# Every second chunk of a stationary-weight block runs its low-half matmuls first

## The chip, the cores and the metric

One NeuronCore of a Trainium2 chip runs the kernel. The metric is the device time of one execution in microseconds. Three runs of the kernel before gave 1018.92, 1020.08 and 1020.14 us; the median is 1020.08 us.

## The reference

The kernel computes one layer of a bidirectional encoder for a sequence of 256 positions and 2048 channels, in float32. The parts that matter here:

```python
h = _rms_norm(x, norm_g)
proj = jnp.einsum('bsd,dn->bsn', h, w_in)          # 2048 -> 16400 columns
q_p, k_p, v_p, o_p, za_p, gif_p, xb_p, zb_p, ga_p, gb_p = jnp.split(proj, cuts, axis=-1)
ya = _mlstm_branch(q_p, k_p, v_p, o_p, za_p, gif_p, b_if, head_g)     # 4 heads
yb = _rglru_branch(xb_p, zb_p, conv_w, conv_b, w_rg, b_rg, lam)       # recurrence over time
ya = jnp.einsum('bsw,wd->bsd', ya, w_branch_a)
yb = jnp.einsum('bsw,wd->bsd', yb, w_branch_b)
merged = sigmoid(ga_p) * ya + sigmoid(gb_p) * yb
return _rms_norm(x + jnp.einsum('bsd,de->bse', merged, w_out), final_g)
```

Nearly all of the work is in the large products. All weights are read once from HBM.

## The kernel before

**Precision by halves.** A float32 product is made of products in a shorter format (fp32r). Each operand is split into a high half (a cast on ScalarE) and a low half (what is left, a subtraction on VectorE). high x high, high x low and low x high are added up in PSUM.

**Chunks.** Weights come in chunks of 128 x 1024 values (512 KB). `load_chunk` issues the DMA on SyncE into a `raw` tile, casts it into a `whi` tile on ScalarE (line 135) and subtracts into a `wlo` tile on VectorE (line 136). There are six `raw` buffers and four each of `whi` and `wlo`. A cast waits until TensorE has done with the `whi` tile of four chunks before.

**The helper that the change touches** is `half_tr` (lines 295 to 309). It makes half a block, 256 transposed output columns, in four chunks (`kq` 0 to 3), with the weights as the stationary operand and the normalised input as the moving one. The input lies in the tile `sHL` with high and low half side by side, 2 x 256 columns for each of 16 slices of the contraction. A chunk has 8 weight tiles of 128 x 128 (4 slices, 2 halves of the output `m`). Before, each chunk runs 8 matmuls with the high halves of the weights (line 302; 512 columns, as they meet both halves of the input) and then 8 with the low halves (line 305; 256 columns, only the input's high half). Here the former are called wide, the latter narrow. Both add into the same PSUM pair `acc`. At the end `fold` (line 311) empties it: a copy on ScalarE (line 315) and an add on VectorE (line 317).

`half_tr` is called 22 times, 88 chunks: for the second to fourth of the query and key blocks (six calls, `qk_block`), for the x-branch of the recurrence in `rg_block(j)` (two calls for each head j, line 667), and for its gate blocks (eight calls, line 881).

**What stands around it.** Heads 0 to 3 come one after the other: `rg_block(j)`, then `head(j)`, which makes the head's v block (`block_nat`, lines 150 to 152) and its o and z blocks (`pair`, lines 166 to 169). Side work is hung between chunks by `tick()`, by lists named in `PLAN`: the convolution, gates and scans of the recurrence (line 736: multiply, 737: multiply, 741 and 743: scans over time), and of the head the product with the scores (line 819), its square and scale (ScalarE line 823, POOL lines 824 and 825, the result `sq`), the multiply with it (VectorE line 826) and the transposes of the result (line 834). Line 799 is a multiply of two gates that this product needs.

**What sets the order.** The Tile framework writes the order of each engine's instructions when the kernel is built: it plays the program through with its own estimate of times and takes, on each engine, what is ready, by priority. Code inside `urgent()` (the loads, casts and subtractions of chunks, and `fold`) has a high priority. On the chip each engine runs its list in that order and waits at semaphores. A change of two loops can therefore move side work on every engine.

Of the kernel before, what the change touches and what calls it, by code (L numbers as in the profile page):

```python
# [15 lines left out]
P = 128  # L16
S = 256
D = 2048
KT = D // P
# [14 lines left out]
            P=('g2 g3',),  # L34
# [12 lines left out]
def hybrid_encoder(ctx: ExitStack, tc: tile.TileContext, x, xt, pk, bif, fg, wg, wi, wr, wa, wb, wo, out):  # L47
    nc = tc.nc
    pe, act, dve, pool, sp = nc.tensor, nc.scalar, nc.vector, nc.gpsimd, nc.sync
# [17 lines left out]
    def sl(tag, dt=F32, cols=4096):  # L67
        return slot.tile([P, cols], dt, tag=tag, name=name("s" + tag))
# [3 lines left out]
    def aux(i=None):  # L72
        if i is None:
            i = auxn[0] % 4
            auxn[0] += 1
        return paux.tile([P, NB], F32, tag=f"aux{i}", name=name("aux"))

    def acc_pair():
        t = pacc.tile([P, 2 * NB], F32, tag="acc", name=name("acc"))
        return [t[:, :NB], t[:, NB:]], t  # L80
# [16 lines left out]
    def tick():  # L97
        if queue:
            c = queue.pop(0)
            if c is not None:  # L100
                c()
        for lane in lanes:
            for c in lane.pop(0) if lane else ():
                c()
# [12 lines left out]
    def load_chunk(src, dst=None, tag="w", bufs=4, parts=1, between=()):  # L117
        with urgent():
            raw = wp.tile([P, KC * NB], F32, tag="raw", name=name("raw"), bufs=6)
            if dst is None:  # L120
                hi = wp.tile([P, KC * NB], F32R, tag=tag + "hi", name=name(tag + "hi"), bufs=bufs)
                lo = wp.tile([P, KC * NB], F32R, tag=tag + "lo", name=name(tag + "lo"), bufs=bufs)
            else:
                hi, lo = dst
            w = KC * NB // parts
            for i in range(parts):
                r = slice(i * w, (i + 1) * w)
                last_dma[0] = (act if between and i == 0 else sp).dma_start(raw[:, r], src[:, r]).ins
                if i == 0:
                    first_dma[0] = last_dma[0]  # L130
            for i in range(parts):
                r = slice(i * w, (i + 1) * w)
                if i < len(between):
                    between[i]()
                last_copy[0] = act.copy(hi[:, r], raw[:, r]).ins  # L135
                last_sub[0] = dve.tensor_sub(lo[:, r], raw[:, r], f(hi[:, r])).ins  # L136
        return hi, lo

    def block_nat(src, xhi, xlo):
        ps, _ = acc_pair()  # L140
        for kq in range(KT // KC):
            tick()
            hi, lo = load_chunk(src[kq])
            for kk in range(KC):
                k = kq * KC + kk
                wh, wl = hi[:, kk * NB:(kk + 1) * NB], lo[:, kk * NB:(kk + 1) * NB]
                for tb in range(2):
                    o = k * S + tb * P
                    a, b = xhi(o, o + P), xlo(o, o + P)
                    pe.matmul(ps[tb], a, wh, start=(k == 0), stop=False)  # L150
                    pe.matmul(ps[tb], a, wl, start=False, stop=False)  # L151
                    pe.matmul(ps[tb], b, wh, start=False, stop=(k == KT - 1))  # L152
        return ps
# [141 lines left out]
    def half_tr(src, half, after=None):  # L295
        ps, both = acc_pair()
        for kq in range(4):
            tick()
            hi, lo = load_chunk(src[half * 4 + kq])
            tiles = [(kq * 4 + kk, m, kk * S + m * P) for kk in range(4) for m in range(2)]  # L300
            for k, m, o in tiles:
                pe.matmul(ps[m], hi[:, o:o + P], hl_t[:, 2 * k * S:2 * (k + 1) * S],  # L302
                          start=(k == 0), stop=False, skip_group_check=True)
            for k, m, o in tiles:
                pe.matmul(ps[m][:, :S], lo[:, o:o + P], hhi(k * S, (k + 1) * S),  # L305
                          start=False, stop=(k == KT - 1), skip_group_check=True)
            if after:
                after(kq)
        return both.rearrange("p (m q s) -> p m q s", m=2, q=2)
# [24 lines left out]
    hl_t = sl("HL", F32R, 8192)  # L334

    def hhi(a, b):
        return hl_t[:, a + a // S * S:a + a // S * S + b - a]
# [251 lines left out]
    def qk_block(blk, key, i, pre=()):  # L589
        ps = block_first(wi[blk], hhi, hlo, pre) if pre else None  # L590
        for m in range(2):
            r = slice(m * NB, (m + 1) * NB)
            if ps:
                v = ps[m]
            else:
                v = hp.tile([P, 2 * NB], F32, tag="to" if m == 0 else "zz", name=name("kt"))[:, :NB]
                fold(v, half_tr(wi[blk], m))
            if m == 0:
                qkh[key] = sl(f"C{i}", F32R, 1024)
                qkl[key] = sl(f"D{i}", F32R, 1024)  # L600
            if key[0] == "k":
                if i == 1:
                    drain_to(r_row)
                with urgent():
                    v3 = v.rearrange("p (m s) -> p m s", m=2)
                    dve.tensor_mul(v3, v3, rbc2)
            evac_split(qkh[key][:, r], qkl[key][:, r], v)
# [57 lines left out]
    def rg_block(j):  # L665
        for i in range(2):
            both = half_tr(wi[BLK_XB + j], i, h_renew if j == 0 and i == 1 else None)
            if j == 0 and i == 1:
                drain()
                rg["hs"] = sl("E")  # L670
            v = xp[:, 2 * i:2 * i + 2, 2:S + 2]
            fold(v, both)
            if j == 0:
                with urgent():
                    dve.tensor_mul(v, v, rbc2)
# [203 lines left out]
    for j in range(4):  # L879
        for i in range(2):  # L880
            both = half_tr(wi[BLK_ZB + j], i)
            if i == 0:
                zt = hp.tile([P, 2 * NB], F32, tag="zz" if j else "vhi", name=name("zt"))
                sg = hp.tile([P, 2 * NB], F32, tag="to" if j else "vlo", name=name("sg"))
            fold(zt[:, i * NB:(i + 1) * NB], both)
        act.activation(sg, zt, AF.Sigmoid)
        dve.tensor_mul(zt, zt, hs[:, j * 1024:(j + 1) * 1024])
        dve.tensor_mul(sg, sg, zt)
        ybh.append(sl(f"C{j}", F32R, 1024))
        ybl.append(sl(f"D{j}", F32R, 1024))  # L890
        act.copy(ybh[j], sg)
        dve.tensor_sub(ybl[j], sg, f(ybh[j]))
        if j == 0:
            fm_t.append(sl("PT", F32R))
        if j == 0:
            drain()
        for kq in (2 * j, 2 * j + 1):
            if kq in k_yb:
                form("b", kq, k_yb.index(kq), full=sg[:, (kq % 2) * NB:(kq % 2 + 1) * NB])
        if j == 1:  # L900
            early[0]()
# [83 lines left out]
    ps = block_nat(wo[2], mh, ml)  # L985
# [21 lines left out]
    for tb, a, b, col in ((0, 0, NB, 3), (1, 0, S, 3), (1, S, NB, 4)):  # L1007
        ps = aux()[:, :b - a]
        for k in range(KT):
            hi, lo = ch[k // KC]  # L1010
            c = (k % KC) * NB
            wh, wl = hi[:, c + a:c + b], lo[:, c + a:c + b]
            o = k * S + tb * P
# [79 lines left out]
```

## Time and profile before

| | |
|---|---|
| median of three runs | 1020.08 us (1018.92 to 1020.14) |
| the profiled execution | 1019.4 us |
| its span, first to last instruction | 1017.7 us |
| TensorE busy | 1009.0 us, 99%, 5076 matmuls |
| VectorE busy | 861.5 us, 85% |
| ScalarE busy | 620.4 us, 61% |
| DMA | 199.34 MB, mean 196 GB/s |

The busy time of a matmul in the trace is its whole way through the array, and matmuls overlap. What one costs in a dense stream is the distance from its start to the start of the next one. In the chain of waits the pieces are set end to end, so there the rows give these distances summed over a run.

### The profile page before, as it was taken

What the parts mean: (1) busy time and instruction counts of PE and PEld (TensorE: products, weight loads), DVE (VectorE), ACT (ScalarE), POOL (GpSimd) and SP (SyncE); (2) the same over time, 40 slices, a digit from 0 to 9 for tenths busy, and PEclk for the clock granted to TensorE, in tenths of its full rate; (3) what the DMA queues carried; (4) which work ended last, traced back from release to release, by engine and by line L of the source; (5) the groups of instructions that cost most, each with busy time, mean ns of one, the idle gap of its engine ahead of it and who ended that gap; (6) DMA issues with size and microseconds to landing.
All of it is one profiled execution on the core that took longest, in us unless ns stands there. A gap on an engine that the chain in (4) does not pass through costs nothing.

```text
span 1017.7 us, 13732 instructions
## 1 busy us (share of the span) xinstructions
PE 1009.0 (99%) x5076; PEld 858.1 (84%) x5076; DVE 861.5 (85%) x1139; ACT 620.4 (61%) x817; POOL 15.9 (2%) x35
## 2 busy tenths in 40 slices
PE   9999999999999999999999999999999999999997
PEld 9988888888888888888888888888888888888886
DVE  6777798689769976997798899997998988999993
ACT  7545476776586759576955565655655656455662
POOL 1000000010001000100000000000000000000000
PEclk9999999999999999999999999999999999999999
DMA  9764545646654566566556556566565656567452
GB/s 355 276 189 142 166 144 190 199 150 191 202 186 165 189 207 184 169 193 214 170 181 211 167 185 228 188 207 205 186 222 195 210 186 206 200 243 290 167 191 83
DMA packets 56100, 199.34 MB, mean 196 GB/s; under 512 B 6368, under 2 KB 6880, under 8 KB 55648
## 3 DMA queue, kind: packets, MB, share of 16 engines
q1 hardware_dynamic: 55168, 197.13, 58.1%
q10 hardware_dynamic: 864, 1.32, 0.4%
q8 instruction: 40, 0.66, 0.3%
q14 instruction: 28, 0.23, 0.1%
HBM read 196.33 MB, written 2.10 MB: 195 GB/s over the span
## 4 chain that ended last, share of the span: by engine, by line
PE 97%; DVE 2%; DMA 1%; issue 0%; ACT 0%; DVEq 0%
PE acc L302 16%; PE acc L166 14%; PE acc L168 14%; PE acc L169 14%; PE acc L305 8%; PE acc L150 4%; PE acc L151 4%; PE acc L152 4%; PE aux L166 3%; PE aux L168 3%; PE aux L169 3%; PE aux L819 1%; PE acc L292 1%; PE acc L290 1%; PE acc L291 1%; PE aux L704 1%
## 5 line engine op out<-in xcount | busy, mean ns | idle before, releaser
L136 DVE TENSOR_TENSOR wlo<-raw,whi 128x1024 fp32r<-128x1024 f32 (+1 forms) x290 | 348.3, 1211 | 82.3 <-ACT whi L135 81.1
L135 ACT CAST whi<-raw 128x1024 fp32r<-128x1024 f32 (+1 forms) x290 | 299.4, 1044 | 191.0 <-PE acc L169 69.4
L302 PE MATMUL acc<-sHL,whi 128*128 128x512 f32 x704 | 178.1, 393 | 0.0
L168 PE MATMUL acc<-wlo,sHL 128*128 128x512 f32 x444 | 173.0, 390 | 0.0
L169 PE MATMUL acc<-whi,sHL 128*128 128x512 f32 x444 | 172.8, 389 | 0.0
L166 PE MATMUL acc<-whi,sHL 128*128 128x512 f32 x444 | 170.6, 389 | 0.0
L302 PEld LDWEIGHTS acc<-sHL,whi 128*128 128x128 f32 x704 | 126.9, 189 | 23.2
L305 PEld LDWEIGHTS acc<-sHL,wlo 128*128 128x128 f32 x704 | 96.0, 190 | 7.2
L305 PE MATMUL acc<-sHL,wlo 128*128 128x256 f32 x704 | 99.2, 283 | 0.0
L166 PEld LDWEIGHTS acc<-whi,sHL 128*128 128x128 f32 x444 | 83.4, 188 | 17.2
L169 PEld LDWEIGHTS acc<-whi,sHL 128*128 128x128 f32 x444 | 83.4, 188 | 17.1
L168 PEld LDWEIGHTS acc<-wlo,sHL 128*128 128x128 f32 x444 | 83.4, 188 | 17.0
L172 ACT CAST whi<-t 128x1024 fp32r<-128x1024 f32 x61 | 64.1, 1052 | 50.7 <-PE acc L169 23.6
L173 DVE TENSOR_TENSOR wlo<-t,whi 128x1024 fp32r<-128x1024 f32 x61 | 74.3, 1219 | 14.0 <-ACT whi L172 13.5
L151 PE MATMUL acc<-wlo,sHL 128*128 128x512 f32 x160 | 62.6, 391 | 0.0
L150 PE MATMUL acc<-whi,sHL 128*128 128x512 f32 x160 | 62.5, 390 | 0.0
L152 PE MATMUL acc<-whi,sHL 128*128 128x512 f32 x160 | 62.4, 390 | 0.0
L173 DVE TENSOR_TENSOR wlo<-raw,whi 128x1024 fp32r<-128x1024 f32 x34 | 41.5, 1221 | 14.7 <-ACT whi L172 14.5
L172 ACT CAST whi<-raw 128x1024 fp32r<-128x1024 f32 x34 | 35.8, 1052 | 27.2 <-PE acc L169 15.7
L172 ACT CAST b<-raw 128x512 fp32r<-128x512 f32 x27 | 16.8, 621 | 34.5 <-DMA raw<-wi 18.9
L168 PE MATMUL acc<-wlo,sA 128*128 128x512 f32 x92 | 36.0, 392 | 0.0
L169 PE MATMUL acc<-whi,sB 128*128 128x512 f32 x92 | 35.9, 390 | 0.0
(363 smaller groups left out, 1694.8 us busy)
## 6 DMA issues: line engine op xcount, KB each, us to landing
raw<-wi SPq DMA_DIRECT2D x254, 512.0 KB, 4.1
raw<-wb SPq DMA_DIRECT2D x32, 512.0 KB, 4.1
raw<-wa SPq DMA_DIRECT2D x32, 512.0 KB, 4.2
raw<-wo SPq DMA_DIRECT2D x32, 512.0 KB, 4.7
raw<-wr SPq DMA_DIRECT2D x8, 512.0 KB, 4.2
sB<-x SPq DMA_DIRECT2D x4, 512.0 KB, 7.8
sA<-x SPq DMA_DIRECT2D x1, 2048.0 KB, 7.7
sA<-xt SPq DMA_DIRECT2D x7, 256.0 KB, 5.5
```

The costliest lines, as they stand in the source:

```text
L135: last_copy[0] = act.copy(hi[:, r], raw[:, r]).ins
L136: last_sub[0] = dve.tensor_sub(lo[:, r], raw[:, r], f(hi[:, r])).ins
L150: pe.matmul(ps[tb], a, wh, start=(k == 0), stop=False)
L151: pe.matmul(ps[tb], a, wl, start=False, stop=False)
L152: pe.matmul(ps[tb], b, wh, start=False, stop=(k == KT - 1))
L166: pe.matmul(ps, a, wh, start=id(ps) not in began, stop=False)
L168: pe.matmul(ps, a, wl, start=False, stop=False)
L169: pe.matmul(ps, b, wh, start=False, stop=stop)
L172: act.copy(hi, v)
L173: dve.tensor_sub(lo, v, f(hi))
L302: pe.matmul(ps[m], hi[:, o:o + P], hl_t[:, 2 * k * S:2 * (k + 1) * S], start=(k == 0), stop=False, skip_group_check=True)
L305: pe.matmul(ps[m][:, :S], lo[:, o:o + P], hhi(k * S, (k + 1) * S), start=False, stop=(k == KT - 1), skip_group_check=True)
```

## The change

The two loops over a chunk's tiles become one, which runs once for the high halves and once for the low halves. For `kq` 0 and 2 the high halves come first, as before; for `kq` 1 and 3 the low halves do. The last matmul into the PSUM pair is now a high one, so `stop` moves there. Nothing else is edited; the code below the place stands two lines further down (line 302 becomes 304, 305 becomes 307, later lines L become L + 2).

```diff
-            for k, m, o in tiles:
-                pe.matmul(ps[m], hi[:, o:o + P], hl_t[:, 2 * k * S:2 * (k + 1) * S],
-                          start=(k == 0), stop=False, skip_group_check=True)
-            for k, m, o in tiles:
-                pe.matmul(ps[m][:, :S], lo[:, o:o + P], hhi(k * S, (k + 1) * S),
-                          start=False, stop=(k == KT - 1), skip_group_check=True)
+            for high in (True, False) if kq % 2 == 0 else (False, True):
+                for k, m, o in tiles:
+                    if high:
+                        pe.matmul(ps[m], hi[:, o:o + P], hl_t[:, 2 * k * S:2 * (k + 1) * S],
+                                  start=(k == 0), stop=(k == KT - 1), skip_group_check=True)
+                    else:
+                        pe.matmul(ps[m][:, :S], lo[:, o:o + P], hhi(k * S, (k + 1) * S),
+                                  start=False, stop=False, skip_group_check=True)
```

In the order that the framework writes, the engines' lists change as follows. The numbers in the names are those of the buffers; `wlo_N+1` is the low half of the chunk whose high half is `whi_N`.

First, TensorE in the gate blocks, two chunks and a half of one half block. Before:

```order
L302 MATMUL acc_5041<-sHL_90,whi_5043 128x512 x8
L305 MATMUL acc_5041<-sHL_90,wlo_5044 128x256 x8
L302 MATMUL acc_5041<-sHL_90,whi_5065 128x512 x8
L305 MATMUL acc_5041<-sHL_90,wlo_5066 128x256 x8
L302 MATMUL acc_5041<-sHL_90,whi_5087 128x512 x8
```

and now:

```order
L304 MATMUL acc_5041<-sHL_90,whi_5043 128x512 x8
L307 MATMUL acc_5041<-sHL_90,wlo_5044 128x256 x8
L307 MATMUL acc_5041<-sHL_90,wlo_5066 128x256 x8
L304 MATMUL acc_5041<-sHL_90,whi_5065 128x512 x8
L304 MATMUL acc_5041<-sHL_90,whi_5087 128x512 x8
```

Narrow runs of two chunks stand side by side, and so do wide ones.

Second, TensorE at the end of the x-branch of head 0, where `acc_2246` is its second half block and `acc_2373` the v block of the head; `to_1961` is the tile whose transposes go to `aux_2471` and `aux_2480`. Before:

```order
L302 MATMUL acc_2246<-sHL_90,whi_2322 128x512 x8
L305 MATMUL acc_2246<-sHL_90,wlo_2323 128x256 x8
L302 MATMUL acc_2246<-sHL_90,whi_2344 128x512 x8
L305 MATMUL acc_2246<-sHL_90,wlo_2345 128x256 x8
L150 MATMUL acc_2373<-whi_2376,sHL_90 128x512
L151 MATMUL acc_2373<-wlo_2377,sHL_90 128x512
```

and now:

```order
L304 MATMUL acc_2246<-sHL_90,whi_2322 128x512 x8
L307 MATMUL acc_2246<-sHL_90,wlo_2323 128x256 x8
L150 MATMUL acc_2373<-whi_2376,sHL_90 128x512
L836 MATMUL aux_2471<-ident,to_1961 128x128
L836 MATMUL aux_2480<-ident,to_1961 128x128
L307 MATMUL acc_2246<-sHL_90,wlo_2345 128x256 x8
L304 MATMUL acc_2246<-sHL_90,whi_2344 128x512 x8
L151 MATMUL acc_2373<-wlo_2377,sHL_90 128x512
```

One matmul of the v block and two transposes now stand ahead of the last chunk, and its low half comes first.

Third, VectorE at the same place. Before:

```order
L743 SCALAR_TENSOR_TENSOR sC_399_1975<-sC_398_1974,sD_400_1976 128x256 x4
L826 SCALAR_TENSOR_TENSOR to_1961<-aux_2138,sq_2132,zz_1962 128x512
L136 TENSOR_TENSOR wlo_2345<-raw_2343,whi_2344 128x1024
L741 SCALAR_TENSOR_TENSOR sE_1524<-sC_319_1648,sE_1524 128x256 x4
L317 TENSOR_TENSOR xp<-acc_2133,fold_2243 128x2x256
L136 TENSOR_TENSOR wlo_2377<-raw_2375,whi_2376 128x1024
```

and now:

```order
L745 SCALAR_TENSOR_TENSOR sC_399_1975<-sC_398_1974,sD_400_1976 128x256 x4
L828 SCALAR_TENSOR_TENSOR to_1961<-aux_2138,sq_2132,zz_1962 128x512
L743 SCALAR_TENSOR_TENSOR sE_1524<-sC_319_1648,sE_1524 128x256 x4
L319 TENSOR_TENSOR xp<-acc_2133,fold_2243 128x2x256
L136 TENSOR_TENSOR wlo_2345<-raw_2343,whi_2344 128x1024
L136 TENSOR_TENSOR wlo_2377<-raw_2375,whi_2376 128x1024
```

The low half `wlo_2345` now stands behind the four scans (lines 741 and 743 of the two versions) and the add that empties the first half block. In heads 1 to 3 the multiply with `sq` (line 826, now 828) has also moved up, ahead of the low half of the second chunk.

## Rows read from the trace of the kernel before

**Rows 1.** The page: the span, and the busy time of each engine with its share of the span and its instructions.

```profile
span 1017.7 us, 13732 instructions
PE 1009.0 (99%) x5076; PEld 858.1 (84%) x5076; DVE 861.5 (85%) x1139; ACT 620.4 (61%) x817; POOL 15.9 (2%) x35
```

**Rows 2.** All waits of TensorE: who waited for whom, us in total, times, longest.

```profile
PE aux L332 <- DVE wu L364: 1.1, 1, 1.1
PE acc L166 <- DVE sD L254: 0.4, 1, 0.4
```

**Rows 3.** TensorE in two windows, the first with wide matmuls alone, the second with narrow ones alone: the window, its length, busy time (matmuls), granted clock, DMA share, GB/s.

```profile
660.00:840.00 180.00, 180.00 (x796) 1.00 0.61 203
7.00:28.00 21.00, 21.00 (x177) 1.00 1.03 403
```

**Rows 4.** The chain of waits through the gate blocks: start, length, and a run of matmuls; the first and the last wide run of 23, and the first narrow one.

```profile
524.24 1.84 PE acc L302 x8
526.08 0.95 PE acc L305 x8
...
585.69 1.84 PE acc L302 x8
```

**Rows 5.** The timeline of TensorE: first and last of 31 wide matmuls in a row, and of 41 narrow ones in a row (start, duration, what it is).

```profile
661.11 0.39 PE L168 MATMUL acc<-wlo,sC 128*128 128x512 f32 x1
...
667.91 0.39 PE L166 MATMUL acc<-whi,sC 128*128 128x512 f32 x1
...
20.14 0.28 PE L290 MATMUL acc<-sHL,whi 128*128 128x256 f32 x1
...
24.94 0.28 PE L291 MATMUL acc<-sHL,whi 128*128 128x256 f32 x1
```

**Rows 6.** Two low halves and the chunks that they are for: in the gate blocks (timeline of VectorE, timeline of TensorE), and in the key blocks (timeline of VectorE, chain of waits).

```profile
521.31 1.21 DVE L136 TENSOR_TENSOR wlo<-raw,whi 128x1024 fp32r<-128x1024 f32 x1
524.07 0.63 PE L302 MATMUL acc<-sHL,whi 128*128 128x512 f32 x2
...
56.42 1.22 DVE L136 TENSOR_TENSOR wlo<-raw,whi 128x1024 fp32r<-128x1024 f32 x1 [1.27 <-ACT whi L135]
65.04 1.84 PE acc L302 x8
```

**Rows 7.** The timeline of VectorE at the end of the x-branch of head 0.

```profile
224.05 2.43 DVE L743 TENSOR_TENSOR_SCAN sC<-sC,sD 128x256 f32<-128x256 f32 x4
226.40 0.72 DVE L826 SCALAR_TENSOR_TENSOR to<-aux,sq,zz 128x512 f32<-128x512 f32 x1
227.04 1.21 DVE L136 TENSOR_TENSOR wlo<-raw,whi 128x1024 fp32r<-128x1024 f32 x1
228.18 2.43 DVE L741 TENSOR_TENSOR_SCAN sE<-sC,sE 128x256 f32<-128x256 f32 x4
230.52 0.66 DVE L317 TENSOR_TENSOR xp<-acc,fold 128x512 f32<-128x512 f32 x1
231.10 1.21 DVE L136 TENSOR_TENSOR wlo<-raw,whi 128x1024 fp32r<-128x1024 f32 x1
```

**Rows 8.** The timeline of TensorE at the same place, and the eight transposes of head 0 with the matmul behind them.

```profile
230.33 2.00 PE L302 MATMUL acc<-sHL,whi 128*128 128x512 f32 x8
...
233.12 0.40 PE L150 MATMUL acc<-whi,sHL 128*128 128x512 f32 x1
233.35 0.40 PE L151 MATMUL acc<-wlo,sHL 128*128 128x512 f32 x1
...
244.03 1.03 PE L834 MATMUL aux<-ident,to 128*128 128x128 f32 x8
244.82 0.37 PE L702 MATMUL aux<-sD,whi 128*128 128x256 f32 x1
```

**Rows 9.** The same place in heads 1, 2 and 3: on VectorE the multiply with `sq` of head 1 and, of each head, the low half of the chunk that follows; on TensorE the wide run of the last chunk (timelines).

```profile
322.13 0.72 DVE L826 SCALAR_TENSOR_TENSOR to<-aux,sq,zz 128x512 f32<-128x512 f32 x1
326.84 1.22 DVE L136 TENSOR_TENSOR wlo<-raw,whi 128x1024 fp32r<-128x1024 f32 x1
326.07 0.86 PE L302 MATMUL acc<-sHL,whi 128*128 128x512 f32 x3
...
422.62 1.21 DVE L136 TENSOR_TENSOR wlo<-raw,whi 128x1024 fp32r<-128x1024 f32 x1
421.84 0.86 PE L302 MATMUL acc<-sHL,whi 128*128 128x512 f32 x3
...
517.80 1.20 DVE L136 TENSOR_TENSOR wlo<-raw,whi 128x1024 fp32r<-128x1024 f32 x1
517.61 0.63 PE L302 MATMUL acc<-sHL,whi 128*128 128x512 f32 x2
```

**Rows 10.** How `sq` of head 1 comes about: the sigmoid on ScalarE, the multiply on VectorE, the square on ScalarE and the two operations on POOL (timelines).

```profile
311.79 1.06 ACT L798 ACTIVATE zz<-zz 128x1024 f32<-128x1024 f32 x1
314.11 1.22 DVE L799 TENSOR_TENSOR zz<-zz,to 128x1024 f32<-128x1024 f32 x1
315.36 0.60 ACT L823 ACTIVATE to<-aux 128x512 f32<-128x512 f32 x1 [0.62 <-DVE zz L799]
...
316.14 0.38 POOL L824 TENSOR_SCALAR sq<-sq 128x1 f32<-128x1 f32 x1 [89.31 <-ACT to L823]
316.60 1.41 POOL L825 TENSOR_TENSOR sq<-sq,mhalf 128x1 f32<-128x1 f32 x1
```

## The prediction

> **What bounds the kernel now.** I read the page's table of engines first: TensorE is busy 1009.0 us of a 1017.7 us span [rows 1]. Then the waits of TensorE: two waits, 1.1 and 0.4 us, are all that the trace holds [rows 2]. So the matmul queue runs almost without a hole, and the time changes only where the change alters the gap between matmuls or opens a hole. The granted clock is the full level, 2.4 GHz, in the windows that I use [rows 3], so no gap below is a matter of the clock.
>
> Next, the chain of waits in the longest stretch of the changed helper. A chunk there is eight wide matmuls (512 columns, line 302) and eight narrow ones (256 columns, line 305). From the wide run that starts at 524.24 to the one at 585.69 there are 22 chunks, so a chunk takes 61.45 / 22 = 2.793 us [rows 4]. Beside it stand long runs of one width: 30 gaps between wide matmuls take 667.91 - 661.11 = 6.80 us, 226.7 ns each, and 40 gaps between narrow ones 24.94 - 20.14 = 4.80 us, 120.0 ns each [rows 5]. Eight of each at these gaps are 1.814 + 0.960 = 2.774 us. What a chunk pays for its two changes of width is therefore 2.793 - 2.774 = 0.020 us. That is all the change can win at a joined pair.
>
> **What it removes.** Counted over the whole order of TensorE, a narrow run is followed by a wide one 72 times before and 43 times after, a wide run by a narrow one 87 times and 43 times; starts of a wide run after anything else (transposes, small products) go from 23 to 8. So 95 - 51 = 44 starts of a wide run go, and as many starts of a narrow run after a wide one: 44 x 0.020 = 0.88 us less. The matmuls themselves (704 and 704), their weight loads, the DMAs and the copies are as many as before, so nothing else is removed.
>
> The trace shows that longer runs are not faster than this: a window with 796 wide matmuls back to back takes 180.00 us, 226 ns each [rows 3]. The Trainium skill ("TensorE: Matmul & The Clock Gate", Back-to-back issue gap) gives N / 2.4 + 2.5 ns for isolated streams, that is 216 ns at 512 columns and 109 ns at 256; here the rows show 227 and 120 in the longest runs, so the sum goes by the rows.
>
> **What it adds: the low half is wanted earlier.** In every second chunk the matmuls with the low half now come first, so the low half, which VectorE makes last (line 136), is wanted 1.84 us sooner, the length of a wide run [rows 4]. The cover is its lead. In the last eight half blocks the shortest lead that I find is at 521.31: the low half is done at 522.52, and its chunk starts at 524.07, 1.55 us later [rows 6]. Most others there have 3 to 7 us; early in the kernel a low half started at 56.42 is done at 57.64 for a chunk at 65.04 [rows 6]. No hole there.
>
> The place without cover is the second half block of the x-branch in each of the four heads, its last chunk. VectorE is back to back there. In head 0 its queue before is: four scans, a multiply, low half of that chunk (227.04, done 228.25), four scans (228.18), an add (230.52), next low half (231.10) [rows 7]. The chunk's high matmuls start at 230.33 [rows 8], so a low half wanted at the start would have had 2.1 us. But the new order of VectorE puts that low half behind the four scans and the add. The block from 227.04 to 231.10 holds the same six pieces of work, now with the low half as the last: it is done at 231.10 + 0.07 = 231.17 (an operation reaches 0.07 us into the next: 227.04 + 1.21 against 228.18). TensorE gets there at 230.33 plus what is put ahead: one matmul of the next block, 0.23 us (233.12 to 233.35), and two transposes, 0.10 us each (eight take 244.03 to 244.82) [rows 8]. 230.33 + 0.43 = 230.76, so a wait of 0.41 us. Heads 1 and 2 have the same order: 326.84 + 0.07 against 326.07 + 0.43 gives 0.41 us, and 422.62 + 0.07 against 421.84 + 0.43 gives 0.42 us. In head 3 the add does not move ahead and two transposes alone come first: 517.80 + 0.07 against 517.61 + 0.20, 0.06 us [rows 9]. Together 1.30 us.
>
> Ends of this term: nothing, if VectorE arrives there half a microsecond earlier than before; or, if it arrives one operation later, 1.14 us more (228.18 - 227.04) in each of four places, 1.30 + 4.56 = 5.9 us. I take 1.3, the nearest to the rows.
>
> A wait here blocks the low run, the wide run behind it and the next block's matmuls, all on TensorE; that queue has no slack, so it goes into the end in full. The new order brings the same kind of small shift to the block after it (one low half of head 0 comes 0.8 us later against a lead of 0.2 us before), but TensorE is late by 0.41 us by then; I give it 0.1 us at most and leave it out. In the first 140 us the order of the gate work changes too. The leads of the chunks there are long [rows 6], and small products move from wide runs into narrow ones at the same count: nothing.
>
> The high half of every second chunk is released 0.95 us later (the length of a narrow run), so ScalarE's cast four chunks on starts later; the copy that empties a half block now stands ahead of one cast. ScalarE is busy 61% [rows 1], and a lead of 7 us falls to some 5.5. That costs nothing; without the cover it would be 0.95 us a chunk. From about 650 us on, all queues have the order of before.
>
> **Sum.** -0.88 + 1.30 = +0.42 us. The profiled execution took 1019.4 us (its span of 1017.7 and 1.7 around it), so 1019.8 on its scale. It lies 0.7 us below the median of the three runs, 1020.08; on the median's scale the forecast is 1020.5 us.
>
> **Rivals.**
> (a) No wait at all: VectorE reaches the late low halves in time, and the joins alone count. 1020.08 - 0.88 = 1019.2. For it: the order puts other matmuls ahead at just these places. Against: 0.41 us still lacks in three heads. Within the same band.
> (b) Slower: VectorE itself is blocked in heads 1 to 3. The multiply with sq (line 826 before), which ran at 322.13 [rows 9], is moved ahead of the second chunk's low half, some 5.6 us earlier. It needs a square on ScalarE and two operations on POOL, which follow a multiply on VectorE (line 799): started 314.11, done 315.33, square 315.36, POOL done 318.01 [rows 10], 2.68 us. The line 799 multiply moves two places ahead, to some 311.9 (it wants the sigmoid, which before ended at 312.85 and now stands one cast of 0.95 us earlier) and ends at 313.1; sq is there at 315.8. Three operations of 1.14 us stand between, so VectorE asks at 316.5: 0.7 us in hand. Each microsecond beyond that delays every low half behind it, and TensorE by as much, in three heads. If the square is held behind two more casts (1.9 us), VectorE stands 1.2 us in each: 3.6 us more, 1020.5 + 3.6 = 1024.1. The point from which it passes the band is 0.6 us of standing in each head.
> (c) Faster: in a run twice as long the second eight matmuls fall to their columns at 2.4 GHz, 213.3 and 106.7 ns, instead of 226.7 and 120.0. 44 x 8 x (13.4 + 13.3) = 9.4 us less: 1011. The formula of the page named above would give nearly that, 7.7 us. Against: the runs of hundreds [rows 3, 5] hold 226 and 120, so this needs something that the trace does not show.
>
> **How the numbers follow.** No change that can be measured means within 0.2%, 2.0 us: 1018.0 to 1022.1. The forecast has 0.63, (a) 0.14, both inside. (b) has 0.18, some of it inside the band and some of the forecast's upper end (a slot of VectorE late) outside: 0.18 slower. (c) has 0.03, and unknown gains from the reordered first 140 us 0.02: faster 0.05, same 0.77. The range runs from (a) less the spread of single runs below it, 1018.8, to the larger part of (b), 1023.4; the forecast's own range is 1019.2 to 1021.8.
>
> **What would show it.** In the profile after: chunks joined, so a pair of chunks in the stretch of 524 to 586 us takes 5.57 instead of 5.59 us; TensorE idle of about 0.4 us ahead of a narrow run with releaser VectorE, line 136, in heads 0 to 2 and next to none in head 3; no wait above 1 us. Waits elsewhere, a VectorE that stands on POOL's sq, or gaps below 220 ns in joined wide runs would make the prediction wrong.

## The result and the profile after

The changed kernel takes 1022.34 us in the median of six runs (1021.37 to 1024.09), the kernel before 1019.36 us in six runs beside them (1018.92 to 1020.14). The ratio is 1.0029 with a 95% interval of 1.0019 to 1.0039: slower by about 3 us. Two single executions in the rounds further down ran at a much lower granted clock than the others (0.75 and 0.85, 1255.86 and 1113.50 us), and the ratios leave them out. The forecast was 1020.5 us, or 0.42 us more than before. The sign was right, the size was not. The time lies inside the wide range of 1018.8 to 1023.4, but outside the forecast's own, 1019.2 to 1021.8.

The page of the changed kernel, span and engines, against [rows 1]:

```profile
span 1022.4 us, 13719 instructions
PE 1011.0 (99%) x5076; PEld 859.8 (84%) x5076; DVE 860.3 (84%) x1139; ACT 619.5 (61%) x817; POOL 17.2 (2%) x35
```

The work is the same: 5076 matmuls, and each engine's busy time within 2 us. The span is 4.7 us longer in this execution, the slowest of the six. The waits of TensorE (who waited for whom, us in total, times, longest), against [rows 2]:

```profile
PE acc L307 <- DVE wlo L136: 2.0, 4, 0.7
```

This line is new: four narrow runs wait for a low half. The others are the two of before (1.1 and 0.6 us) and one of 0.4 us on line 292 at the very start of the program, which comes and goes between executions. The four places in the timeline of TensorE (start, duration, what it is, idle time before and its releaser), against [rows 8, 9]:

```profile
232.24 0.38 PE L836 MATMUL aux<-ident,to 128*128 128x128 f32 x2
232.96 1.22 PE L307 MATMUL acc<-sHL,wlo 128*128 128x256 f32 x8 [0.34 <-DVE wlo L136]
234.02 2.00 PE L304 MATMUL acc<-sHL,whi 128*128 128x512 f32 x8
...
328.58 0.38 PE L836 MATMUL aux<-ident,to 128*128 128x128 f32 x2
329.64 1.21 PE L307 MATMUL acc<-sHL,wlo 128*128 128x256 f32 x8 [0.68 <-DVE wlo L136]
330.69 2.00 PE L304 MATMUL acc<-sHL,whi 128*128 128x512 f32 x8
...
425.29 0.38 PE L836 MATMUL aux<-ident,to 128*128 128x128 f32 x2
426.34 1.22 PE L307 MATMUL acc<-sHL,wlo 128*128 128x256 f32 x8 [0.67 <-DVE wlo L136]
427.39 2.00 PE L304 MATMUL acc<-sHL,whi 128*128 128x512 f32 x8
...
521.75 0.38 PE L836 MATMUL aux<-ident,to 128*128 128x128 f32 x2
522.44 1.22 PE L307 MATMUL acc<-sHL,wlo 128*128 128x256 f32 x8 [0.31 <-DVE wlo L136]
523.50 3.82 PE L304 MATMUL acc<-sHL,whi 128*128 128x512 f32 x16
```

The idle time in brackets is not the whole price. It is counted only from the end of the last matmul on its way through the array, so the distances between starts say more. From the two transposes to the narrow run behind them it is 0.72, 1.06, 1.05 and 0.69 us. Where two transposes come without a wait, the next start follows after 0.14 us:

```profile
247.00 0.38 PE L836 MATMUL aux<-ident,to 128*128 128x128 f32 x2
247.14 0.36 PE L704 MATMUL aux<-sD,whi 128*128 128x256 f32 x1
```

So 0.58 + 0.92 + 0.91 + 0.55 = 2.96 us are lost in the waits. The narrow run itself then takes 1.05 or 1.06 us to the next start, where one in a stream takes 0.95 [rows 4]. That tenth is not a price of the wait alone, because a run behind transposes has it without a wait too. Sixteen narrow matmuls behind six transposes take 2.00 us here and not 1.91, and in the kernel before eight wide ones behind eight transposes take 1.93 us and not 1.84:

```profile
527.16 0.82 PE L836 MATMUL aux<-ident,to 128*128 128x128 f32 x6
527.73 2.16 PE L307 MATMUL acc<-sHL,wlo 128*128 128x256 f32 x16
529.73 3.82 PE L304 MATMUL acc<-sHL,whi 128*128 128x512 f32 x16
...
521.19 2.09 PE L302 MATMUL acc<-sHL,whi 128*128 128x512 f32 x8
523.12 1.11 PE L305 MATMUL acc<-sHL,wlo 128*128 128x256 f32 x8
```

Before, the eight transposes of a head stood in one group with one such tenth; now they stand in two or three groups, each of them shorter, with a tenth behind each. That is 0.1 us more in all four heads together. Waits and groups together cost 3.1 us.

VectorE at the same place of head 0 and of head 1, against [rows 7, 9]:

```profile
225.78 2.43 DVE L745 TENSOR_TENSOR_SCAN sC<-sC,sD 128x256 f32<-128x256 f32 x4
...
228.77 2.43 DVE L743 TENSOR_TENSOR_SCAN sE<-sC,sE 128x256 f32<-128x256 f32 x4
...
231.69 2.35 DVE L136 TENSOR_TENSOR wlo<-raw,whi 128x1024 fp32r<-128x1024 f32 x2
...
319.04 0.74 DVE L828 SCALAR_TENSOR_TENSOR to<-aux,sq,zz 128x512 f32<-128x512 f32 x1
...
323.11 2.43 DVE L745 TENSOR_TENSOR_SCAN sC<-sC,sD 128x256 f32<-128x256 f32 x4
...
328.38 2.34 DVE L136 TENSOR_TENSOR wlo<-raw,whi 128x1024 fp32r<-128x1024 f32 x2
```

Two low halves now stand in a row behind both groups of scans, and the first of the two is the one that TensorE stands for. VectorE has no idle time there: the multiply with `sq` (line 828) of head 1 runs at 319.04 with nothing in brackets.

The joins, in the chain of waits through the gate blocks, against [rows 4]:

```profile
529.89 3.65 PE acc L304 x16
533.54 1.91 PE acc L307 x16
...
579.99 3.65 PE acc L304 x16
```

From 529.89 to 579.99 there are nine pairs of chunks, 50.10 / 9 = 5.567 us each. Before it was 2 x 2.793 = 5.586.

One more thing sets this execution apart, in a window of 4 us early in the program (window, its length, busy time and matmuls, weight loads, VectorE, ScalarE, POOL, granted clock, DMA share, GB/s):

```profile
98.00:102.00 4.00, 4.00 (x16) 3.44 (x16) 3.36 (x7) 1.29 (x5) 0.00 (x0) 0.61 0.59 180
```

The granted clock is 0.61 here and 0.53 from 98.7 to 102.2 us, where the engine ran at the lower level, 1.2 GHz. Summed over the starts in the trace that is about 1.6 us, and this execution, at 1024.09 us, stands 1.75 above the median of its six. It is told apart below.

### The profile page after: what moved, and what is told of

It reads as the page before. It is cut to its first block, busy times and chain, and to the rows that moved or that the text cites. A ratio compares the mean times of both kernels' runs of the same rounds, so it can differ in the third digit from the quotient of the medians.

```text
span 1022.4 us, 13719 instructions
## 1 busy us (share of the span) xinstructions
PE 1011.0 (99%) x5076; PEld 859.8 (84%) x5076; DVE 860.3 (84%) x1139; ACT 619.5 (61%) x817; POOL 17.2 (2%) x35
## 4 chain that ended last, share of the span: by engine, by line
PE 90%; DVE 5%; ACT 2%; issue 1%; DMA 1%; ACTq 0%; DVEq 0%; SPq 0%
PE acc L168 14%; PE acc L166 14%; PE acc L169 14%; PE acc L304 13%; PE acc L307 7%; PE acc L151 4%; PE acc L152 4%; PE acc L150 3%; PE aux L166 3%; PE aux L168 3%; PE aux L169 3%; DVE wlo L136 1%; DVE sE L743 1%; DVE sC L745 1%; PE aux L705 1%
## 5 line engine op out<-in xcount | busy, mean ns | idle before, releaser
L304 PE MATMUL acc<-sHL,whi 128*128 128x512 f32 x704 | 170.1, 392 | 0.0
L304 PEld LDWEIGHTS acc<-sHL,whi 128*128 128x128 f32 x704 | 129.9, 189 | 25.1
L307 PE MATMUL acc<-sHL,wlo 128*128 128x256 f32 x704 | 97.1, 286 | 2.0 <-DVE wlo L136 2.0
L307 PEld LDWEIGHTS acc<-sHL,wlo 128*128 128x128 f32 x704 | 92.4, 192 | 7.6 <-DVE wlo L136 2.9
L317 ACT COPY fold<-acc 128x512 f32<-128x512 f32 x22 | 12.9, 587 | 45.9 <-PE acc L304 45.9
```

## The experiments

Two theories stood at first. **W**: the loss is the four waits, 3.1 us with what comes behind each, less 0.9 us of joins; they arise where a low half is wanted first and VectorE has put it last. **R**: the loss lies elsewhere, in the reordered first 140 us, in the fall of the clock, or in the low-first order as such. Seven kernels ran, each in five rounds beside the kernel before. In most, the helper's two orders were made a parameter:

```diff
-    def half_tr(src, half, after=None):
+    def half_tr(src, half, after=None, low_first=(1, 3)):
...
-            for high in (True, False) if kq % 2 == 0 else (False, True):
+            for high in (False, True) if kq in low_first else (True, False):
```

One correction first. The expectations, like the prediction, put all four places into the x-branch. The lists show that three lie there: the last chunk of the second half block of the x-branches that run beside the rest of heads 0, 1 and 2. The fourth, beside the rest of head 3, is the last chunk of the second half block of the first gate block.

**The changed kernel again**, unedited.

> The changed kernel again, unedited, as the base for the other runs. Theory W (the time was lost in the four waits on VectorE's low half at the last chunk of the second x half block, about 3.2 us with the restart behind each, less 0.9 us of joins): the four waits on line 136 are there again, 1.7 to 2.3 us of idle time in all, and the ratio to before is 1.0022 to 1.003. Theory R (the time was lost elsewhere: the reordered side work of the first 140 us, the fall of the clock near 98 us, or the low-first order by itself): the granted clock falls again near 98 us in the profiled execution.

Measured: 1021.63 against 1019.37 us, ratio 1.0025 (1.0016 to 1.0034). Its waits have the same first line (2.0 us, four times, longest 0.7). Its early window reads:

```profile
98.00:102.00 4.00, 4.00 (x22) 3.42 (x23) 2.90 (x6) 1.49 (x4) 0.00 (x0) 1.00 0.60 201
```

The four waits are there to the tenth; the clock is at its full level. So the fall is no part of the loss that remains without it: 2.26 us between the medians, against 3.1 - 0.9 = 2.2 from the four places and the joins.

**The waited chunk high first again.** The last chunk of every second x half block:

```diff
-            both = half_tr(wi[BLK_XB + j], i, h_renew if j == 0 and i == 1 else None)
+            both = half_tr(wi[BLK_XB + j], i, h_renew if j == 0 and i == 1 else None,
+                           low_first=(1,) if i else (1, 3))
```

> As the changed kernel, but the last chunk of the second x half block of each head runs high first again. VectorE still makes that chunk's low half behind the scans; TensorE needs it 1.8 us later. Theory W: no wait on line 136 at the four places, and what is left are the joins: ratio 0.9990 to 0.9996 (-0.4 to -1.0 us). Theory R: the ratio stays at 1.002 or more.

Measured: ratio 1.0038 (1.0025 to 1.0052). W missed, since it said faster. R's number came (1.002 or more), and in this profile the granted clock fell again in the early window (0.61). But the waits show where most of the loss is:

```profile
PE acc L151 <- DVE wlo L136: 3.0, 3, 1.3
...
PE acc L307 <- DVE wlo L136: 0.3, 1, 0.3
```

Three of the four waits are gone, as W said (the fourth, 0.3 us, is the one in the gate block, which this edit does not reach). Three longer ones have come up in the v block (line 151), some 15 us later. TensorE there in head 0:

```profile
247.89 0.39 PE L150 MATMUL acc<-whi,sHL 128*128 128x512 f32 x1
248.84 0.50 PE L151 MATMUL acc<-wlo,sHL 128*128 128x512 f32 x1 [0.55 <-DVE wlo L136]
```

and the chain of waits that leads to it:

```profile
239.49 1.15 DVE wlo L136
...
240.66 4.47 DMA raw<-wi
...
245.22 0.63 DVE xp L191
245.85 0.40 DVE sD L691
246.25 0.60 DVE sB L173
246.86 0.79 DVE sD L688 x2
247.65 1.15 DVE wlo L136
```

Read from below: the v block's low half stands on VectorE behind the additions of the next pair of blocks (lines 191, 173), these wait for a weight transfer, and the transfer waited for a buffer that a low half gave back when it ended, 239.49 + 1.15 = 240.64. In the kernel before the same places read (VectorE):

```profile
237.89 1.21 DVE L136 TENSOR_TENSOR wlo<-raw,whi 128x1024 fp32r<-128x1024 f32 x1
...
243.73 0.69 DVE L191 TENSOR_TENSOR xp<-raw 128x512 f32<-128x512 f32 x1 [0.64 <-DMA raw<-wi]
...
245.13 1.22 DVE L136 TENSOR_TENSOR wlo<-raw,whi 128x1024 fp32r<-128x1024 f32 x1
```

The clock times can't be compared as they stand, because this whole program is 1.5 us later here: its first matmul of the v block starts at 234.60, that of before at 233.12. Counted from there, the transfer starts after 6.06 us here and 6.01 before, and line 191 starts after 10.62 and 10.61, so buffer and transfer are as they were. The list behind line 191 is not. Before, the low half starts 1.40 us after line 191; two small operations stand between. Here line 173 and three small operations stand between, and it starts 2.34 us after (247.56 against 245.22 in the timeline). That 0.94 us makes the wait: before, the low half had a lead of 0.2 us there. In heads 1 and 2 the same 0.94 us is in the list, and besides the buffer comes back 0.4 us later and the transfer lands later.

In the changed kernel that low half stands directly behind line 191:

```profile
246.31 0.68 DVE L191 TENSOR_TENSOR xp<-raw 128x512 f32<-128x512 f32 x1
246.92 1.21 DVE L136 TENSOR_TENSOR wlo<-raw,whi 128x1024 fp32r<-128x1024 f32 x1
```

It is done 0.7 us before TensorE wants it at 248.88 (line 151), so there is no wait. At the place where the changed kernel waits, VectorE has the same order in both; in the v block the two lists differ. So each version has a list of its own, and TensorE stands at whichever low half that list has too late. I call this theory **O**, against **L**, that low first at the waited chunk is what costs.

**Only the waited chunk low first**, all else as before; `low_first` is empty elsewhere:

```diff
+                           low_first=(3,) if i else ())
```

> As the kernel before, but the last chunk of the second x half block of each head runs low first; four chunks in the program. In this program the low half of that chunk stands ahead of the scans in VectorE's list, as before. Theory W, in the form that VectorE's order makes the wait: no wait above 0.1 us at the four places, ratio 0.9995 to 1.0005. Rival, that low first at this chunk is dear whatever VectorE's order: four waits and +2 to +3 us, ratio 1.002 to 1.003.

Measured: ratio 0.9997 (0.9989 to 1.0006). VectorE at head 0:

```profile
227.31 1.22 DVE L136 TENSOR_TENSOR wlo<-raw,whi 128x1024 fp32r<-128x1024 f32 x1
228.44 2.43 DVE L744 TENSOR_TENSOR_SCAN sE<-sC,sE 128x256 f32<-128x256 f32 x4
```

and TensorE:

```profile
229.63 2.08 PE L307 MATMUL acc<-sHL,wlo 128*128 128x256 f32 x16
```

With the low half ahead of the second scans, as before, the very chunk that waits in the changed kernel runs low first without a wait: sixteen narrow matmuls in a row, the last eight from 230.58 on, 2 us after their operand. L falls.

**The scan one step later.** The changed kernel, with the first scan step of the x blocks hung one chunk later:

```diff
-            X=('e0 m0', 'e1', '', 'r0 r1', 's1', 's0 m1', 'y'),
+            X=('e0 m0', 'e1', '', 'r0 r1', 's1', 'm1', 's0 y'),
```

> As the changed kernel with all its low-first chunks, but the first scan step of the x blocks hangs one chunk later in the list of side work, so that on VectorE the low half of the last chunk stands behind a multiply and an add and no longer behind four scans. Theory W: the four waits go or fall below 0.2 us each, ratio 0.9990 to 0.9998; what the scans do one step later may cost a few tenths of a us. Theory R: ratio 1.002 or more.

Measured: 1018.95 against 1019.37 us, ratio 0.9999 (0.9991 to 1.0008), just above what W said. Of its two waits one is new:

```profile
PE aux L836 <- DVE to L828: 0.5, 1, 0.5
```

The only other one is the 1.1 us at the start that before has too [rows 2]. All low-first chunks are in, no narrow run waits, and the loss is gone: what W and O say, and not what R says of the low-first order. The step has a price of its own: in head 3 the transposes (line 836) wait 0.5 us for a multiply that now stands behind the scans. The span, 1017.0 us, is 0.7 below that of before: 0.9 from the joins less that wait, within the spread of single executions.

**What sets the new order.** The order that the framework writes with single chunks flipped tells it: to make the *last chunk of the first half block* low first is enough to move the scans ahead of the low half in the *next* half block (why the framework does so was not followed). This edit alone, four chunks, none of them at a waited place:

```diff
+                           low_first=() if i else (3,))
```

> As the kernel before, but the last chunk of the first x half block of each of the four x branches runs low first: four chunks in the program, none of them at a place where the changed kernel waits. This alone gives VectorE the order of the changed kernel behind it: four scans ahead of the next block's last low half, then two low halves in a row. Theory O (the loss comes from the order in which VectorE's list has the low halves and the scans, whichever half a chunk starts with): TensorE waits on line 136 in heads 0 to 2 as in the run with the last chunk high first again, at the third chunk of the v block, 2.5 to 3.5 us in all, and the ratio to before is 1.0025 to 1.004. Theory L (low first at the waited chunk is what costs): no such waits, ratio 0.9995 to 1.0005.

Measured: ratio 1.0038 (1.0024 to 1.0052), as O said. Waits:

```profile
PE acc L151 <- DVE wlo L136: 2.9, 3, 1.4
```

VectorE in head 0, at the low half of the waited chunk of the changed kernel and ahead of the longest wait, which ends at 248.55:

```profile
227.22 2.43 DVE L744 TENSOR_TENSOR_SCAN sE<-sC,sE 128x256 f32<-128x256 f32 x4
...
230.15 2.35 DVE L136 TENSOR_TENSOR wlo<-raw,whi 128x1024 fp32r<-128x1024 f32 x2
...
244.94 0.69 DVE L191 TENSOR_TENSOR xp<-raw 128x512 f32<-128x512 f32 x1 [1.61 <-DMA raw<-wi]
...
247.28 1.22 DVE L136 TENSOR_TENSOR wlo<-raw,whi 128x1024 fp32r<-128x1024 f32 x1
```

The scans stand ahead of the two low halves, and in the v block the chain is that of the run with the waited chunk high first, without a single low-first chunk where TensorE waits. (It is the fifth chunk of the v block; the expectation said the third.) Four flipped chunks cost about as much as all forty-four do: the changed kernel has the joins on its credit side, and a list without the late low half in the v block.

How much of a wait is the list and how much the transfer can be read in head 0. From line 191 to the low half it is again 2.34 us, the 0.94 more than before. The transfer took 5.5 us from its issue at 239.31, a microsecond more than above, and TensorE stands 1.60 us between starts instead of 0.72. So the list alone makes a wait of 0.7 us there, and a late transfer comes on top. Over the six places of the two runs it is 4.4 to 5.6 us from the issue of the transfer to line 191; why it varies is not shown.

**The joins with the old order.** Everything low first as in the changed kernel, except the first x half blocks, the waited chunks, and the first gate half block:

```diff
+                           low_first=(1,) if i else ())
...
-            both = half_tr(wi[BLK_ZB + j], i)
+            both = half_tr(wi[BLK_ZB + j], i, low_first=(1, 3) if j + i else ())
```

> As the changed kernel, but the chunks of the first x half blocks, the last chunk of the second x half blocks and the first gate half block run high first as before. VectorE then has the order of before at all four places, and 34 of the 44 joined starts are left. Theory O: no wait on line 136 above 0.1 us there, and 34 x 0.020 = 0.7 us less than before: span 1016.7 to 1017.4 where before has 1017.7, ratio 0.9988 to 1.0000. Theory R (the reordered first 140 us costs by itself): 1.001 or more, with the granted clock below 1.00 near 98 us.

Measured: ratio 0.9997 (0.9988 to 1.0006), span 1017.2 us, inside what O said. No wait on line 136 is left in the heads. The waits of this run are the 1.1 us at the start that before has too and the 0.4 us on line 292.

**Query and key blocks alone** low first in every second chunk (`low_first=(1, 3)` there, empty elsewhere).

> As the kernel before, but every second chunk of the query and key blocks runs low first; from the x branches on everything is as before. Theory O: no wait on line 136 in the heads; 8 to 12 joins, so -0.2 us: ratio 0.9993 to 1.0003. Theory R: the first 140 us are what costs, ratio 1.001 to 1.002, or the granted clock falls near 98 us as in the changed kernel's first profile.

Measured: ratio 0.9996 (0.9986 to 1.0005), span 1016.9 us. No narrow run waits, and the granted clock in the early window is 1.00. So the reordered first 140 us cost nothing that shows, and with the repeated run and the one with the later scan R falls in all its forms. The run with the old order, the one with the later scan and this one lie 0.4 to 0.8 us below before in their medians, where 0.2 to 0.9 was expected of the joins, and every interval holds 1: no version here is shown to beat the kernel before.

## Why the prediction was right or wrong

**The joins, -0.88 us: right.** A pair of chunks takes 5.567 us where 5.57 was said; a joined wide run takes 3.65 us instead of 2 x 1.84, a joined narrow one 1.91 instead of 2 x 0.95.

**Longer runs no faster per matmul, rival (c): refuted.** 3.65 / 16 is 228 ns and 1.91 / 16 is 119 ns, close to the gaps of [rows 5]. The 216 and 109 ns that the Trainium skill ("TensorE: Matmul & The Clock Gate", Back-to-back issue gap) gives for isolated matmuls are not reached here either.

**Where the waits are: right in kind.** The prediction read from the order of VectorE that the low half of four chunks goes behind the scans, and all four waits are there, with the releaser that it named. In heads 0 to 2 the instructions ahead are those it named; in head 3 it expected next to no wait, and there are 0.31 us of idle time. In head 0 its arithmetic holds: it had VectorE ready 7.12 us after the scans began and TensorE there after 6.71; measured are 231.69 + 1.20 - 225.78 = 7.11 and 232.24 + 0.20 - 225.78 = 6.66.

**Their size, "together 1.30 us": the step that failed.** It is 3.1 us. The largest part is TensorE's arrival in heads 1 to 3. Counted in head 1 from the start of the first scans (319.79 before), the prediction's 326.91 for VectorE and 326.50 for TensorE, both less 0.65 for the multiply that went ahead of the scans, are 7.12 - 0.65 = 6.47 and 6.71 - 0.65 = 6.06 us. Measured are 328.38 + 1.20 - 323.11 = 6.47 and 328.58 + 0.20 - 323.11 = 5.67. VectorE is where it was expected, TensorE 0.39 us sooner against it. Head 2 gives the same two numbers to 0.02 us, and in head 3, where 0.06 was said and 0.49 came on this count, TensorE is 0.39 us sooner as well. The way from the second chunk to the place is as long as before (5.56 us, 320.51 to 326.07 and 322.79 to 328.35), so TensorE was sooner already when the second chunk began. The trace shows what left the stretch ahead of that: of the six products with the scores, three have gone to an earlier place (the stretch, its length, busy time and count of these matmuls, weight loads, granted clock, DMA share, GB/s):

```profile
319.12:320.51 1.39, 1.38 (x6) 0.95 (x6) 1.00 0.81 312
...
322.08:322.78 0.70, 0.69 (x3) 0.40 (x3) 1.00 0.67 246
```

It is so in heads 1 to 3, the three with the 0.39 us; in head 0 all six are still there, and there the arithmetic held. How the 0.69 us of these three comes down to 0.39 was not followed. "Heads 1 and 2 have the same order" was therefore the wrong reading: the prediction had counted the matmuls put ahead of the chunk, and not those taken away from the way to it. The rest of the difference is small terms in each place: 0.06 us between the end of the operand and the first start, 0.06 us because two transposes take 0.14 and not 0.20 us, and 0.1 us in all for the transposes in more groups.

**What costs nothing, the first 140 us and the late release of the high half: right** as far as shown, by the run with the query and key blocks alone and by the ScalarE that appears in no wait of TensorE; the fall of the clock in some executions stays open. **Rival (a), no wait,** is what the runs with the later scan and with the old order are, not the changed kernel. **Rival (b), VectorE blocked by the multiply with `sq`:** not seen; that multiply ran at 319.04 without idle time before it. The point "no wait above 1 us" held. The v block, which the prediction left out, costs nothing in the changed kernel; but the low half with a lead of 0.2 us that it saw there is the one at which two of the other versions wait.

**Luck.** By the prediction's own line of 0.2% the result is slower, which it gave 0.18, and gave that mainly to rival (b). The range reaches to 1023.4 because of (b), which did not happen. That the time lies inside it is luck; the forecast's own upper end was 1021.8.

**The cause** was told too narrowly. The heading of that step, the low half is wanted earlier, is true of the changed kernel but not needed: the run with four flipped chunks elsewhere loses as much. What matters is that VectorE's list has a low half too late, and flips elsewhere are enough to bring that about.

**The sum** with the measured terms is -0.9 + 3.1 = +2.2 us; the repeated run gives +2.26, the first measurement +2.98, and the intervals of both (1.0016 to 1.0034, 1.0019 to 1.0039) hold it.

## What to carry to other kernels

Where a scheduler writes the queues, a local swap is to be judged by what it does to the lists of the engines that feed the bottleneck: here a swap in one block moved scans ahead of operands in the next, and undoing the swap at the place of the wait gave another list, with a late operand 15 us further on. When two versions are compared, count times from a common piece of work: a clock time of the one may be 1.5 us off in the other. Compare the feeder's lateness, the time from a fixed piece of its work to the wanted operand, with the bottleneck's own way to that place, and recount both sides, since the bottleneck may come earlier too. And price a wait by the distances between starts, not by its idle time: here 2.0 us of idle time were 3.0 us between starts.

## What was not expected of the hardware

A run behind transposes takes 0.1 us longer, whether TensorE waited or not: 1.05 or 1.06 us instead of 0.95 for eight narrow matmuls behind the four waits, 2.00 instead of 1.91 for sixteen and 1.93 instead of 1.84 for eight wide ones without a wait. Behind the waits of the v block, where no transposes stand, the first matmul takes as much longer (248.84 to 249.17, 0.33 us, where the next ones take 0.23). The cause is not shown, and the loss shows in no row of the waits.

In the changed kernel's first profile and in the one with the waited chunk high first, the granted clock was 0.61 between 98 and 102 us, after narrow runs with small side products (lines 569 and 570) between them. Four other profiles with the same low-first query and key blocks had 1.00 there, so the fall comes in some executions only. Whether the changed order makes it likelier stays open: with two in six here and none in the three profiles with the old order there, the count is too small.
